# Squared activations of two MLPs: both halves in one buffer, at chosen offsets, and side by side in the second layer

## The chip, the core and the metric

The kernel runs on one core of a Trainium2 chip. The metric is the time of one execution on the device in microseconds (us). Times are read from one profiled execution, and the kernel was timed in further runs without that profile.

## What is computed

The reference is a decoder trunk of two layers on 256 tokens of width 1024, in float32. The first layer mixes tokens by trailing means over 2 to 16 positions, the second by causal attention; both add attention to a memory of 256 rows, and each ends in an MLP with a squared ReLU. Cut to what matters here:

```
for i in range(DEPTH):                       # 2 layers
    u = rms_norm(x, g_mix[i])
    ...                                      # token mixer and memory attention
    x = x + concatenate([tok, mo]) @ w_out[i]
    u = rms_norm(x, g_mlp[i])
    x = x + square(relu(u @ w_ff1[i])) @ w_ff2[i]   # 1024 -> 4096 -> 1024
```

## The kernel before

Every matrix product is done in three parts to keep float32 accuracy. An operand is held as two tiles: `hi`, the value rounded to the type `float32r`, and `lo`, what is left of it. `mm3` (L125 to L128) then adds hi·hi, hi·lo and lo·hi in an accumulator. Weights come from HBM into raw tiles of 512 KB; `split` (L113) makes `hi` on ScalarE (L118, L121) and `lo` on VectorE (L119, L122), 128 partitions by 512 columns each, in a pool of 16 tiles of either kind.

An MLP (`mlp`, L399) works through the 4096 hidden columns in eight groups `g` of 512. `ff1(g)` multiplies the slices of `w_ff1` as stationary operand with the transposed input (`x1T` in the first layer, `x3T` in the second): eight matmuls of 512 columns (L426) and eight of 256 (L428) for each 128 hidden columns. `square` (L402) folds two such accumulators (ScalarE's copy `c` at L407, VectorE's sum `r` at L408), squares the positive part into `h` (L411), rounds it to `hh` on ScalarE (L412) and writes the rest `hl` on VectorE (L413). Each of `hh` and `hl` holds 512 columns: two blocks of 128 hidden units by 256 tokens.

`ff2(g)` multiplies them with `w_ff2`. Here a slice of 128 tokens of `hh` or `hl` is the stationary operand, loaded before each matmul, and 512 columns of the weights are the moving one. A group has 4 hidden blocks × 2 blocks of tokens × 2 halves of the output × 3 parts = 48 matmuls; TensorE loads `hh` for the first two parts (L126, L127) and `hl` for the third (L128). The order on TensorE is ff1(0), ff1(1), ff2(0), ff1(2), ff2(1) and so on, so a group's `hh` and `hl` are written about one group before they are read.

Where tiles lie: `hi`, `lo`, `x1T`, `x3T`, `hh` and `hl` all begin at the same remainder of 512 bytes within a partition, since their sizes are multiples of 512 bytes and a filler tile of 96 values (L232) precedes the pools that hold `hh` and `hl`. Each has 4 buffers of 2048 bytes for `hh` and as many for `hl`, used in turn, so a buffer is written again two groups later.

Of the kernel before, what the change touches and what calls it, by code (L numbers as in the profile page):

```python
# [11 lines left out]
F32R = mybir.dt.float32r  # L12
# [6 lines left out]
P = 128  # L19
# [14 lines left out]
QG, KG = 58, 122  # L34
NSMALL = 186
NWARM = 7
LAG = 2

PLAN = {'x': 6, 'q': 5, 'bw': 7, 'pool': 5, 'mem0': (1, 3, 6, 6),
# [14 lines left out]
def trunk(ctx: ExitStack, tc: tile.TileContext, x, mem, x_t0, x_t, mem_t, small, bands, rope, mask,  # L54
# [13 lines left out]
    def nm(s):  # L68
        uid[0] += 1
        return f"{s}_{uid[0]}"  # L70

    def psum(name="ps"):
        return psp.tile([P, 512], F32, tag="ps", name=nm(name))

    def accum():
        return accp.tile([P, 512], F32, tag="acc", name=nm("acc"))
# [20 lines left out]
    wps = psum("warm")  # L97
    for _ in range(NWARM):
        nc.tensor.matmul(wps, warm[:, :P], warm, start=True, stop=True)
# [3 lines left out]
    def load_raw(src):  # L103

        n = src.shape[1]
        k = src.shape[0] // P
        r = rawp.tile([P, k, n], F32, tag="raw", name=nm("raw"))
        nc.sync.dma_start(r, src.rearrange("(k p) n -> p k n", p=P))
        return r
# [3 lines left out]
    def split(raw, g=None):  # L113
        n = raw.shape[-1]
        hi = wp.tile([P, n], F32R, tag="hi", name=nm("hi"))
        lo = wp.tile([P, n], F32R, tag="lo", name=nm("lo"))
        if g is None:
            nc.scalar.activation(hi, raw, AF.Copy)  # L118
            nc.vector.tensor_tensor(lo, raw, hi.bitcast(F32), op=ALU.subtract)  # L119
        else:  # L120
            last_hi[0] = nc.scalar.activation(hi, raw, AF.Copy, scale=g)  # L121
            nc.vector.scalar_tensor_tensor(lo, raw, g, hi.bitcast(F32), op0=ALU.mult, op1=ALU.subtract)  # L122
        return hi, lo

    def mm3(o, a, b, start, stop):  # L125
        nc.tensor.matmul(o, a[0], b[0], start=start, stop=False)  # L126
        nc.tensor.matmul(o, a[0], b[1], start=False, stop=False)  # L127
        nc.tensor.matmul(o, a[1], b[0], start=False, stop=stop)  # L128
# [20 lines left out]
    def big_t(name):  # L149

        t = tp.tile([P, NKC, 2, S], F32R, tag="t", name=nm(name))
        return t[:, :, 0, :], t[:, :, 1, :], t
# [125 lines left out]
    def later(fn):  # L278
        pend.append(fn)
        while len(pend) > LAG:  # L280
            pend.pop(0)()
# [108 lines left out]
    def mlp_stats():  # L390
        e2 = []
        for b in range(2):
            ms = norm_stats(xr[:, b, :], f"mlp{b}")
            r2 = st.tile([P, 1], F32, tag=f"r2{b}", name=nm("r2"))
            nc.vector.reciprocal(r2, ms)
            e2.append(r2)
        return e2

    def mlp(l, t, hp, finish):  # L399
        acc = []  # L400

        def square(zs, hh, hl):  # L402

            z = hp.tile([P, 2, S], F32, tag="r", name=nm("r"), bufs=2)
            for i in range(2):
                c = hp.tile([P, S], F32, tag="c", name=nm("c"), bufs=2)
                nc.scalar.activation(c, zs[i][:, S:], AF.Copy)  # L407
                nc.vector.tensor_tensor(z[:, i, :], zs[i][:, :S], c, op=ALU.add)  # L408
            z = z.rearrange("p i t -> p (i t)")
            h = hp.tile([P, 512], F32, tag="h", name=nm("h"), bufs=2)  # L410
            nc.vector.scalar_tensor_tensor(h, z, 0.0, z, op0=ALU.max, op1=ALU.mult)  # L411
            nc.scalar.activation(hh, h, AF.Copy)  # L412
            nc.vector.tensor_tensor(hl, h, hh.bitcast(F32), op=ALU.subtract)  # L413

        def ff1(g):
            pieces = []
            for q in range(4):
                raw = load_raw(w_ff1[l][q * 256:(q + 1) * 256, g * 512:(g + 1) * 512])
                for j in range(2):
                    k = 2 * q + j  # L420
                    pieces.append(split(raw[:, j, :], sm[:, GMLP + 8 * l + k:GMLP + 8 * l + k + 1]))

            def steps(o, n, ks):

                for k in ks:
                    nc.tensor.matmul(o, pieces[k][0][:, n * P:(n + 1) * P], t[2][:, k, :, :], start=k == 0, stop=False)  # L426
                for k in ks:
                    nc.tensor.matmul(o[:, :S], pieces[k][1][:, n * P:(n + 1) * P], t[0][:, k, :],  # L428
                                     start=False, stop=k == NKC - 1)

            res = [(hp.tile([P, 512], F32R, tag="hh", name=nm("hh"), bufs=4),
                    hp.tile([P, 512], F32R, tag="hl", name=nm("hl"), bufs=4)) for _ in range(2)]
            if g == 0:
                z = [accum() for _ in range(4)]
                for k0 in (0, 4):
                    for n in range(4):
                        steps(z[n], n, range(k0, k0 + 4))
                for i in range(2):
                    square(z[2 * i:2 * i + 2], *res[i])
                return res  # L440
            for i in range(2):
                z = [psum("step") for _ in range(2)]
                for n in range(2):
                    steps(z[n], 2 * i + n, range(NKC))
                square(z, *res[i])
            return res

        def ff2(g, hs):
            last = g == 7
            if g == 0:  # L450
                acc.extend([[accum(), accum()], [accum(), accum()]])
            held = []

            def go(b, h, f, pieces):
                hh, hl = hs[f // 2]
                o = (f % 2) * S + b * P
                mm3(acc[b][h], (hh[:, o:o + P], hl[:, o:o + P]), pieces[h], g == 0 and f == 0, last and f == 3)

            for f in range(4):
                raw = load_raw(w_ff2[l][g * 512 + f * P:g * 512 + (f + 1) * P, :])  # L460
                held.append([split(raw[:, 0, h * 512:(h + 1) * 512]) for h in range(2)])
                if not last:
                    for b in range(2):
                        for h in range(2):
                            go(b, h, f, held[f])
            if last:
                for h in range(2):
                    for b in range(2):
                        for f in range(4):
                            go(b, h, f, held[f])  # L470
                        finish(b, h, acc[b][h])

        prev = ff1(0)
        r2.extend(mlp_stats())
        for g in range(1, 8):
            cur = ff1(g)
            ff2(g - 1, prev)
            prev = cur
        ff2(7, prev)
# [11 lines left out]
    with tc.tile_pool(name="l0", bufs=1) as lp:  # L491
# [15 lines left out]
        for k in range(0, NKC, 2):  # L507
# [11 lines left out]
            for j in range(2):  # L519
                if k == 0 and j == 1:  # L520
                    evac_split(xt0[:, S:2 * S], xT[0][:, 1, :], xT[1][:, 1, :])
                g = xt0[:, 2 * S + j:2 * S + j + 1] if k == 0 else sm[:, GMIX + k + j:GMIX + k + j + 1]
                p = split(raws[j], g)
# [43 lines left out]
        dhi, dlo, _ = big_t("d")  # L567
# [59 lines left out]
        for l in range(2):  # L627
            g = cp.tile([P, 1], F32, tag=f"mg{l}", name=f"mg{l}")
# [45 lines left out]
    with tc.tile_pool(name="l1", bufs=1) as lp:  # L674
# [6 lines left out]
        for i, (gc, f) in enumerate(((QG, 1.0), (KG, 8.0))):  # L681
            for b in range(2):
                cc, ss = rp[:, b, 0, :], rp[:, b, 1, :]
                g1, g2 = sm[:, gc:gc + 32], sm[:, gc + 32:gc + 64]
                for j, (g, src, sg) in enumerate(((g1, cc, f), (g2, cc, f), (g2, ss, -f), (g1, ss, f))):
                    nc.vector.scalar_tensor_tensor(tcs[:, b, j // 2, i, (j % 2) * 32:(j % 2) * 32 + 32],
                                                   g, sg, src, op0=ALU.mult, op1=ALU.mult)
# [187 lines left out]
```

## Time and profile before

| | us |
|---|---|
| median of 3 timed runs | 562.98 |
| lowest and highest of them | 562.65, 562.99 |
| profiled execution | 562.31 |
| its span, first to last instruction | 560.5 |
| TensorE busy in the span | 552.2 |
| VectorE busy | 397.6 |
| ScalarE busy | 343.2 |

The first layer's MLP fills about 93 to 275 us of the span, the second layer's 376 us to the end. In the rows below PE is TensorE's matmul, PEld its load of a stationary operand (which overlaps matmuls), DVE is VectorE, ACT ScalarE, POOL GpSimd. [...] Names are those of the program, out<-in, with buffer numbers left out.

### The profile page before, as it was taken

What the parts mean: (1) busy time and instruction counts of PE and PEld (TensorE: products, weight loads), DVE (VectorE), ACT (ScalarE), POOL (GpSimd) and SP (SyncE); (2) the same over time, 40 slices, a digit from 0 to 9 for tenths busy, and PEclk for the clock granted to TensorE, in tenths of its full rate; (3) what the DMA queues carried; (4) which work ended last, traced back from release to release, by engine and by line L of the source; (5) the groups of instructions that cost most, each with busy time, mean ns of one, the idle gap of its engine ahead of it and who ended that gap; (6) DMA issues with size and microseconds to landing.
All of it is one profiled execution on the core that took longest, in us unless ns stands there. A gap on an engine that the chain in (4) does not pass through costs nothing.

```text
span 560.5 us, 8156 instructions
## 1 busy us (share of the span) xinstructions
PE 552.2 (99%) x2883; PEld 459.6 (82%) x2883; DVE 397.6 (71%) x795; ACT 343.2 (61%) x658; POOL 24.5 (4%) x27
## 2 busy tenths in 40 slices
PE   7999999999999999999999999999999999999997
PEld 5888788888888888888878777888888888888885
DVE  5888977784765856847969999667768477486542
ACT  6879966574563753755766887656637546466330
POOL 0202110000000000000012112000000000000000
PEclk9999999999999999999999999999999999999999
DMA  8988763645836637549473343355374483574301
GB/s 296 355 307 291 232 195 132 196 142 185 255 122 225 195 146 260 161 143 295 132 229 113 108 143 118 116 178 160 114 262 143 160 291 111 198 238 135 117 0 75
DMA packets 46408, 101.94 MB, mean 182 GB/s; under 512 B 3488, under 2 KB 11168, under 8 KB 46368
## 3 DMA queue, kind: packets, MB, share of 16 engines
q1 hardware_dynamic: 46224, 101.17, 55.5%
q8 instruction: 22, 0.36, 0.3%
q10 hardware_dynamic: 144, 0.26, 0.1%
q14 instruction: 18, 0.15, 0.1%
HBM read 100.37 MB, written 1.05 MB: 181 GB/s over the span
## 4 chain that ended last, share of the span: by engine, by line
PE 91%; DVE 3%; ACT 2%; POOL 1%; DMA 1%; issue 1%; ACTq 0%; DVEq 0%
PE step L426 18%; PE acc L126 18%; PE acc L127 18%; PE acc L128 18%; PE step L428 10%; PE acc L426 3%; PE av_out L342 1%; PE acc L428 1%; PE exp_t L306 1%; POOL r L172 1%; PE transpose L145 1%; PE tok_scores L723 1%; ACT hi L121 1%; DMA raw<-in_w_in_pool_dram 1%; DVE lo L122 1%
## 5 line engine op out<-in xcount | busy, mean ns | idle before, releaser
L122 DVE SCALAR_TENSOR_TENSOR lo<-raw,sm,hi 128x512 fp32r<-128x512 f32 x210 | 149.4, 749 | 31.6 <-ACT hi L121 18.1
L121 ACT ACTIVATE hi<-raw,sm 128x512 fp32r<-128x512 f32 x210 | 139.6, 718 | 32.3 <-PE acc L128 29.9
L118 ACT ACTIVATE hi<-raw 128x512 fp32r<-128x512 f32 (+1 forms) x152 | 92.2, 628 | 45.8 <-PE acc L128 40.5
L119 DVE TENSOR_TENSOR lo<-raw,hi 128x512 fp32r<-128x512 f32 (+1 forms) x152 | 97.2, 689 | 19.7 <-ACT hi L118 19.7
L126 PE MATMUL acc<-hi,hh 128*128 128x512 f32 x256 | 99.9, 390 | 0.0
L128 PE MATMUL acc<-hi,hl 128*128 128x512 f32 x256 | 99.8, 390 | 0.0
L127 PE MATMUL acc<-lo,hh 128*128 128x512 f32 x256 | 99.8, 390 | 0.0
L408 DVE TENSOR_TENSOR r<-step,c 128x256 f32<-128x256 f32 x56 | 23.7, 423 | 57.7 <-ACT c L407 57.7
L407 ACT ACTIVATE c<-step 128x256 f32<-128x256 f32 x56 | 21.3, 380 | 68.8 <-PE step L428 68.8
L128 PEld LDWEIGHTS acc<-hi,hl 128*128 128x128 f32 x256 | 48.1, 188 | 10.0
L426 PE MATMUL step<-x1T,hi 128*128 128x512 f32 x224 | 55.9, 392 | 0.0
L426 PE MATMUL step<-x3T,hi 128*128 128x512 f32 x224 | 55.9, 392 | 0.0
L126 PEld LDWEIGHTS acc<-hi,hh 128*128 128x128 f32 x256 | 48.1, 188 | 9.5
L127 PEld LDWEIGHTS acc<-lo,hh 128*128 128x128 f32 x256 | 48.1, 188 | 9.5
L426 PEld LDWEIGHTS step<-x3T,hi 128*128 128x128 f32 x224 | 40.7, 189 | 7.5
L426 PEld LDWEIGHTS step<-x1T,hi 128*128 128x128 f32 x224 | 40.7, 189 | 7.5
L428 PEld LDWEIGHTS step<-x3T,lo 128*128 128x128 f32 x224 | 30.6, 190 | 2.2
L428 PEld LDWEIGHTS step<-x1T,lo 128*128 128x128 f32 x224 | 30.5, 190 | 2.2
L126 PE MATMUL acc<-hi,x2T 128*128 128x512 f32 x80 | 32.1, 401 | 0.0
L128 PE MATMUL acc<-hi,x2T 128*128 128x512 f32 x80 | 31.7, 396 | 0.0
L127 PE MATMUL acc<-lo,x2T 128*128 128x512 f32 x80 | 31.6, 395 | 0.0
L428 PE MATMUL step<-x3T,lo 128*128 128x256 f32 x224 | 31.2, 282 | 0.0
(155 smaller groups left out, 778.3 us busy)
## 6 DMA issues: line engine op xcount, KB each, us to landing
raw<-in_w_ff_dram SPq DMA_DIRECT2D x128, 512.0 KB, 4.8
raw<-in_w_out_dram SPq DMA_DIRECT2D x16, 512.0 KB, 4.4
raw<-in_w_in_moba_dram SPq DMA_DIRECT2D x24, 256.0 KB, 4.2
raw<-in_w_mem_kv_dram SPq DMA_DIRECT2D x8, 512.0 KB, 4.6
raw<-in_w_in_moba_dram SPq DMA_DIRECT2D x8, 512.0 KB, 4.8
raw<-in_w_in_pool_dram SPq DMA_DIRECT2D x7, 512.0 KB, 6.5
xr<-in_x_dram SPq DMA_DIRECT2D x2, 512.0 KB, 8.2
raw<-in_mem_t_dram SPq DMA_DIRECT2D x4, 256.0 KB, 6.6
```

The source lines that it names most:

```text
L118: nc.scalar.activation(hi, raw, AF.Copy)
L119: nc.vector.tensor_tensor(lo, raw, hi.bitcast(F32), op=ALU.subtract)
L121: last_hi[0] = nc.scalar.activation(hi, raw, AF.Copy, scale=g)
L122: nc.vector.scalar_tensor_tensor(lo, raw, g, hi.bitcast(F32), op0=ALU.mult, op1=ALU.subtract)
L126: nc.tensor.matmul(o, a[0], b[0], start=start, stop=False)
L127: nc.tensor.matmul(o, a[0], b[1], start=False, stop=False)
L128: nc.tensor.matmul(o, a[1], b[0], start=False, stop=stop)
L145: nc.tensor.transpose(ps[:, c * P:(c + 1) * P], src[:, (c0 + c) * P:(c0 + c + 1) * P], ident)
L407: nc.scalar.activation(c, zs[i][:, S:], AF.Copy)
L408: nc.vector.tensor_tensor(z[:, i, :], zs[i][:, :S], c, op=ALU.add)
L426: nc.tensor.matmul(o, pieces[k][0][:, n * P:(n + 1) * P], t[2][:, k, :, :], start=k == 0, stop=False)
L428: nc.tensor.matmul(o[:, :S], pieces[k][1][:, n * P:(n + 1) * P], t[0][:, k, :], start=False, stop=k == NKC - 1)
```

## The change

The two tiles become one of 9 × 128 values (4608 bytes), one for each of the four buffers `j` = 2·(g mod 2) + i. Within it the halves begin at an offset from the table `RES`, in bytes.

In the first layer (`l` = 0) `hh` is 512 contiguous columns at that offset and `hl` the next 512; the four offsets are 224, 160, 16 and 240 bytes. In the second layer (`l` = 1) the buffer is 512 pairs: `hh` takes the even places and `hl` the odd ones, so that the two halves of a value lie side by side, and neighbouring columns of `hh` are 8 bytes apart; the offsets are 0, 64, 128 and 192 bytes. Since a buffer's size is a multiple of 512 bytes and its pool begins where it did, these offsets are also the distances from the remainder at which the weights begin.

```
+RES = (224, 160, 16, 240, 0, 64, 128, 192)
...
-            res = [(hp.tile([P, 512], F32R, tag="hh", name=nm("hh"), bufs=4),
-                    hp.tile([P, 512], F32R, tag="hl", name=nm("hl"), bufs=4)) for _ in range(2)]
+            res = []
+            for i in range(2):
+                j = 2 * (g % 2) + i
+                u = hp.tile([P, 9 * P], F32R, tag=f"hb{j}", name=nm("hb"), bufs=1)
+                o = RES[4 * l + j] // 4
+                if l:
+                    w = u[:, o:o + 1024].rearrange("p (n two) -> p n two", two=2)
+                    res.append((w[:, :, 0], w[:, :, 1]))
+                else:
+                    res.append((u[:, o:o + 512], u[:, o + 512:o + 1024]))
```

The instructions of each engine stand in the same order as before, with the same shapes, and each waits for the same engines. What differs is the addresses of `hh` and `hl`, and in the second layer the step of two elements with which ScalarE and VectorE write them, VectorE reads `hh` at L413, and TensorE loads them.

## Rows read from the trace of the kernel before

**Rows 1.** the page: busy us of each engine, and the granted clock in tenths

```profile
span 560.5 us, 8156 instructions
...
PE 552.2 (99%) x2883; PEld 459.6 (82%) x2883; DVE 397.6 (71%) x795; ACT 343.2 (61%) x658; POOL 24.5 (4%) x27
...
PEclk9999999999999999999999999999999999999999
```

**Rows 2.** who TensorE waited for, whole span: us in total, times, longest us

```profile
PE acc L126 <- ACT hi L121: 1.6, 1, 1.6
PE mem_kv_finish L255 <- DVE kn L242: 1.3, 2, 0.8
PE warm L99 <- DVE warm L94: 1.2, 1, 1.2
```

**Rows 3.** the chain of work that ended last, shares of the span by engine

```profile
PE 91%; DVE 3%; ACT 2%; POOL 1%; DMA 1%; issue 1%; ACTq 0%; DVEq 0%
```

**Rows 4.** groups by line in the second MLP, 376 to 560.5 us: TensorE

```profile
line engine op names shapes xcount | busy us, mean ns | idle before us <-releasers
...
L127 PEld LDWEIGHTS acc<-lo,hh 128*128 128x128 f32 x128 | 24.1, 188 | 4.7
L126 PEld LDWEIGHTS acc<-hi,hh 128*128 128x128 f32 x128 | 24.1, 188 | 4.8
L128 PEld LDWEIGHTS acc<-hi,hl 128*128 128x128 f32 x128 | 24.0, 188 | 5.0
```

**Rows 5.** timeline of TensorE's matmuls around one ff2 block: start us, us, instruction, count

```profile
503.37 1.12 PE L428 MATMUL step<-x3T,lo 128*128 128x256 f32 x8
504.32 2.00 PE L426 MATMUL step<-x3T,hi 128*128 128x512 f32 x8
506.16 1.12 PE L428 MATMUL step<-x3T,lo 128*128 128x256 f32 x8
...
512.70 0.40 PE L126 MATMUL acc<-hi,hh 128*128 128x512 f32 x1
...
514.09 0.39 PE L126 MATMUL acc<-hi,hh 128*128 128x512 f32 x1
...
523.38 0.39 PE L128 MATMUL acc<-hi,hl 128*128 128x512 f32 x1
523.61 1.98 PE L426 MATMUL step<-x3T,hi 128*128 128x512 f32 x8
```

**Rows 6.** timeline of TensorE's weight loads in that block

```profile
514.09 0.19 PEld L127 LDWEIGHTS acc<-lo,hh 128*128 128x128 f32 x1
```

**Rows 7.** timeline of TensorE, a matmul beside which nothing is loaded

```profile
339.18 0.39 PE L126 MATMUL acc<-hi,x2T 128*128 128x512 f32 x1
...
339.38 0.20 PEld L710 LDWEIGHTS qk_evac<-ident,rot 128*128 128x128 f32 x2 [0.23 <-ACT hi L118]
339.41 0.41 PE L710 MATMUL qk_evac<-ident,rot 128*128 128x128 f32 x2
```

**Rows 8.** groups by line in the second MLP: ScalarE and VectorE

```profile
L118 ACT ACTIVATE hi<-raw 128x512 fp32r<-128x512 f32 x64 | 39.2, 630 | 21.8 <-PE acc L128 19.2 <-PE acc L426 1.9
...
L413 DVE TENSOR_TENSOR hl<-h,hh 128x512 fp32r<-128x512 f32 x16 | 11.1, 691 | 5.0 <-ACT hh L412 4.9
...
L412 ACT ACTIVATE hh<-h 128x512 fp32r<-128x512 f32 x16 | 10.0, 628 | 9.1 <-DVE h L411 9.1
```

**Rows 9.** busy us of each engine in the two MLPs' stretches

```profile
core 0: us, PE busy (x) PEld busy (x) DVE busy (x) ACT busy (x) POOL busy (x), PEclk, DMA share, GB/s
...
376.00:560.50 184.50, 180.70 (x919) 153.77 (x917) 114.55 (x193) 93.31 (x170) 0.00 (x0) 1.00 0.47 155
```

**Rows 10.** timelines of VectorE and TensorE: the last hl, and its buffer's first reader

```profile
538.72 0.69 DVE L413 TENSOR_TENSOR hl<-h,hh 128x512 fp32r<-128x512 f32 x1
...
545.66 0.39 PE L126 MATMUL acc<-hi,hh 128*128 128x512 f32 x1
...
547.02 0.39 PE L126 MATMUL acc<-hi,hh 128*128 128x512 f32 x1
```

## The prediction

> **What bounds the kernel now.** I read the busy shares first. TensorE is busy for 552.2 of 560.5 us, at the full granted clock in every slice, with VectorE at 71% and ScalarE at 61% [rows 1]. Busy does not yet mean bound, so the second view is the list of what TensorE waited for: three entries, 4.1 us in total, on lines 99, 126 and 255, and at none of them is a squared activation the operand waited for [rows 2]. The chain that ended last is TensorE for 91% of the span [rows 3]. So only an edit that alters the spacing of matmuls can move the end by much, and the question is what this one does to that spacing.
>
> The change touches two kinds of instruction in each MLP: ScalarE's and VectorE's writes of the two halves (`hh` at L412, `hl` at L413, 16 each per layer), and the weight loads of the second matrix product, in which a 128-column slice of `hh` or `hl` is the stationary operand (L126 to L128). There are 384 of these per layer: 256 with `hh`, 128 with `hl` [rows 4]. Each is followed by one matmul of 512 columns. No engine's order and no kind of wait changes, so there is no moved step to price, only durations and what lies behind them.
>
> **How fast the product runs now.** In the timeline of TensorE I take the starts of one block of 48 of these matmuls [rows 5]. From 514.09 to 523.38 there are 41 intervals: 9.29 us / 41 = 226.6 ns each. The first six intervals, from 512.70 to 514.09, come straight after the shorter matmuls of L428 and take 1.39 us, or 231.7 ns each. The whole block, 512.70 to 523.61, takes 10.91 us; 48 × 226.6 = 10.88. Only 0.03 us of a block is above its own steady pace.
>
> Is 226.6 ns a floor, or is it itself the result of weight loads that get in the way of the matmul being streamed? At 339.18 a 512-column matmul of L126 starts, and the next weight load begins only at 339.38, since it waited for another engine; the next matmul starts at 339.41 [rows 7]. The interval is 0.23 us although nothing was loaded for the first 0.20 us of it. The same 0.23 with and without a load beside it: I take 226.6 ns as the matmul's own time. That limits the gain: 16 blocks × 0.03 us = 0.5 us, under 0.1% of the time.
>
> **How much room a weight load has.** The load of the next matmul is issued when the present one starts (514.09 for both) [rows 5, 6]. The 256-column matmuls of L428 show how long a load keeps its unit occupied: eight of them, each with a load of its own, start at 503.37 and the next group at 504.32 [rows 5], 0.95 us / 8 = 119 ns. A load therefore occupies at most 119 ns, although the records show about 190 ns for one [rows 4], a length that evidently overlaps its successor. Under a 512-column matmul it has 226.6 − 119 = 108 ns to spare.
>
> **The edits, one by one.**
> (a) Second layer, stride of two elements in 384 weight loads. The trace has no weight load with a stride. Lower bound of its cost: nothing, if the load takes up to 1.9 times as long (226.6 / 119), because it stays under the matmul. Upper bound: a load of twice the length, 238 ns, then sets the interval: (238 − 226.6) × 384 = 4.4 us. I take nothing, since the spare time covers all but a full doubling. What the cover hides is 384 × 119 = 46 us of loading.
>
> [...]
>
> (b) First layer, 384 contiguous loads whose buffers begin 224, 160, 16 and 240 bytes off the grid of 512 bytes on which all weight tiles and, so far, all of `hh` and `hl` begin. Slices now differ by multiples of 512 bytes, and the steady block [rows 5] runs through all of them at one pace; nothing in the trace shows a finer offset. Lower bound: all stalls after L428 vanish, −0.25 us (8 blocks × 0.03). Upper bound: every matmul pays what the first six of a block pay, 231.7 − 226.6 = 5.1 ns, × 384 = 2.0 us. I take nothing: 41 of 47 intervals of the block are at the floor.
>
> [...]
>
> (c) ScalarE's and VectorE's strided writes in the second layer: 16 × 628 ns and 16 × 691 ns now [rows 8]. Between unchanged and doubled, this adds 0 to 10.0 us on ScalarE and 0 to 11.1 us on VectorE. In 376 to 560.5 us they are busy 93.31 and 114.55 of 184.5 us [rows 9], so even doubled they stay at 103 and 126. The cover is the distance between writing and reading: the last `hl` of the kernel is written at 538.72 and its buffers are first read seven matmuls into the block from 545.66, at 547.02 [rows 10], some 7.6 us later; all other buffers have at least the block in between. Behind these instructions on their queues stand the splits of weights (L118, L119) and the copies that free the accumulators (L407); ScalarE waits for TensorE there, 19.2 us in front of L118 in this stretch [rows 8], and TensorE never for it in the MLP [rows 2]. Taken at nothing. Should the cover go, the cost would be the 0.7 us of the last such instruction, once.
>
> (d) One buffer for both halves in place of two: it is reused two groups later, as before; no new wait.
>
> **Sum.** The profiled execution took 562.31 us, 1.8 us more than its span of 560.5; the median of the three timed runs is 562.98, 0.67 above it. Terms: 0 + 0 + 0 + 0, with ends of −0.5 and +6.4 us. Forecast: 563.0 us.
>
> **Rivals.**
> R1, slower: offsets decide whether a load and a matmul that run together stall. Place: the 384 pairs of the first layer, and perhaps those of the second, where the load now walks through memory twice as fast. Price: the 231.7 ns of the first six intervals as a lasting pace, 2.0 us per layer; by the eight L426 matmuls after L428 (504.32 to 506.16, 1.84 us / 8 = 230 ns) 1.3 us. So 564.3 to 565.0 for one layer, up to 567.0 for both. It decides once the stall lasts instead of dying out. For it: stalls exist, with the same instructions, and depend on something as fine as the moment of a load's start. Against: they die out within six matmuls.
> R2, slower: the strided load takes about twice as long, 4.4 us in the second layer alone: 567.4. It decides from 226.6 ns on. For it: twice as many bytes are passed over for the same 128 columns. Against: the 108 ns of room.
> [...]
> R4: the edit does nothing, because the addresses do not matter and the stride is free. That is the forecast itself.
>
> **How the numbers follow.** Forecast (with R4) 0.51, R1 0.28, R2 0.16, R3 0.05. A measurement of this kernel tells about 0.2%, or 1.1 us, from no change. Faster by more 0.05 (R3; the 0.5 us of stalls is not enough), within 0.2% 0.51, slower 0.44 (R1 and R2). The range runs from 562.3 (the forecast with every stall gone) to 567.2, which takes in R1 whole and most of R2, and leaves out R3 and the upper end of R2, some 0.13.
>
> **What would show it.** [...] The durations of L412 and L413 in the second layer show (c), and the list of TensorE's waits must still have no entry on L126 to L128 for `hh` or `hl`. The forecast is wrong if either layer's blocks of 48 take more than 10.95 us each, or if a wait for L412 or L413 appears on TensorE.

## The result and the profile after

The changed kernel takes 566.50 us (median of 4 runs, 566.12 to 567.63) against 562.97 us for the kernel before (4 runs, 562.65 to 562.99): a ratio of 1.0072 with a 95% interval of 1.0058 to 1.0085, 3.5 us slower. That lies in the range, but the central forecast, no change, was wrong. What happened is the rival R1, in both layers: in the first by the offsets, in the second already by the stride.

The page of the kernel after, its parts on busy time, the granted clock and the chain that ended last:

```profile
span 565.8 us, 8156 instructions
...
PE 557.5 (99%) x2883; PEld 463.2 (82%) x2883; DVE 397.6 (70%) x795; ACT 343.2 (61%) x658; POOL 24.5 (4%) x27
...
PEclk9999999999999999999999999999999999999999
...
PE 91%; DVE 3%; ACT 2%; POOL 1%; DMA 1%; issue 1%; ACTq 0%; DVEq 0%
```

Beside [rows 1, 3] only TensorE differs. VectorE and ScalarE are busy exactly as long as before, the granted clock shows as full in every slice, the chain has the same shares. TensorE is busy 5.3 us longer with the same 2883 matmuls, and the span has grown by the same 5.3 us.

Who TensorE waited for in the kernel after (us in total, times, longest):

```profile
PE acc L129 <- ACT hi L124: 1.7, 1, 1.7
PE mem_kv_finish L258 <- DVE kn L245: 1.3, 2, 0.8
PE warm L102 <- DVE warm L97: 1.2, 1, 1.2
```

These are the three entries of [rows 2], three lines further down in the code (L126 to L128 are now L129 to L131, L426 is L429, L412 and L413 are L415 and L416). There is no new wait. Matmuls with nothing to wait for stand further apart. (A matmul recorded at 0.39 us at 523.38 is followed by the next at 523.61 [rows 5]; in a stream one costs the distance between two starts, here 0.23 us.)

Where? Timelines of TensorE, first and last matmul of either MLP (first of L429, last of L131), after:

```profile
96.31 1.08 PE L429 MATMUL acc<-x1T,hi 128*128 128x512 f32 x4
...
276.39 0.39 PE L131 MATMUL acc<-hi,hb 128*128 128x512 f32 x1
...
382.99 1.08 PE L429 MATMUL acc<-x3T,hi 128*128 128x512 f32 x4
...
561.64 0.39 PE L131 MATMUL acc<-hi,hb 128*128 128x512 f32 x1
```

and the same four in the kernel before:

```profile
94.79 1.07 PE L426 MATMUL acc<-x1T,hi 128*128 128x512 f32 x4
...
272.93 0.40 PE L128 MATMUL acc<-hi,hl 128*128 128x512 f32 x1
...
379.60 1.08 PE L426 MATMUL acc<-x3T,hi 128*128 128x512 f32 x4
...
556.31 0.39 PE L128 MATMUL acc<-hi,hl 128*128 128x512 f32 x1
```

The first MLP takes 180.08 us instead of 178.14, the second 178.65 instead of 176.71: 1.94 us more in each. The other 1.5 us by which the profiled spans differ had passed before the first MLP began (96.31 against 94.79). That stretch is not touched by the change. In the eight runs below that leave it alone as well, the MLP began between 1.2 us earlier and 0.8 us later than in the trace of before, whatever the edit. What differs lies in the first 13 us. TensorE starts the first projection at 6.0 us before and 6.1 us after and runs on without a pause; its 512-column matmuls stand 0.43 us apart at first, up to 8.7 us before and up to 12.2 us after, and 0.23 us from then on. (The trace's records of the granted clock begin, at full, at 8.9 us before and at 12.2 us after; what it was until then no record shows, and the page counts that time as full.) Eight intervals more at 0.43 us cost 1.6 us. That is probably why the profiled execution, at 567.63, is the longest of the four. The comparisons that decide below use the length of an MLP or of one block, which this start does not enter.

Within the MLPs it is almost all in the second product: the intervals that start with one of its matmuls add up to 1.79 us more in the first layer and 1.85 in the second. The rest is in the L429 matmuls (229.4 to 230.2 and 229.9 ns). Timelines of TensorE after: one `ff2` block in the second layer, then one in the first.

```profile
517.28 0.40 PE L129 MATMUL acc<-hi,hb 128*128 128x512 f32 x1
517.52 0.40 PE L130 MATMUL acc<-lo,hb 128*128 128x512 f32 x1
...
528.44 0.85 PE L429 MATMUL step<-x3T,hi 128*128 128x512 f32 x3
```

```profile
119.13 0.39 PE L129 MATMUL acc<-hi,hb 128*128 128x512 f32 x1
...
130.32 0.86 PE L429 MATMUL step<-x1T,hi 128*128 128x512 f32 x3
```

From the first row of a block to the L429 behind it are 48 matmuls: 11.16 us here against 10.91 in [rows 5], and 11.19 in the first layer. The blocks alternate, since even and odd groups use different buffers: 11.19 and 11.10 us in the first layer, 11.10 and 11.16 in the second. Over the six full blocks of a layer the intervals average 233.3, 233.0, 233.4 and 228.9 ns for the first layer's buffers (offsets 224, 160, 16 and 240) and 232.8, 229.9, 231.9 and 233.2 for the second's (0, 64, 128 and 192). So a pace like that of the first six matmuls of a block before (231.7 ns) now holds through most blocks to the end. The exception is the buffer at 240, the second half of this block:

```profile
141.50 0.39 PE L129 MATMUL acc<-hi,hb 128*128 128x512 f32 x1
...
147.11 0.39 PE L129 MATMUL acc<-hi,hb 128*128 128x512 f32 x1
...
152.60 0.62 PE L429 MATMUL step<-x1T,hi 128*128 128x512 f32 x2
```

At offset 16 the first 24 matmuls take 5.61 us, 233.8 ns each; at 240 the other 24 take 5.49 us, 228.8 ns each.

### The profile page after: what moved, and what is told of

Its sections match the earlier page's. It is cut to its first block, busy times and chain, and to the rows that moved or that the text cites. A ratio compares the mean times of both kernels' runs of the same rounds, so it can differ in the third digit from the quotient of the medians.

```text
span 565.8 us, 8156 instructions
## 1 busy us (share of the span) xinstructions
PE 557.5 (99%) x2883; PEld 463.2 (82%) x2883; DVE 397.6 (70%) x795; ACT 343.2 (61%) x658; POOL 24.5 (4%) x27
## 4 chain that ended last, share of the span: by engine, by line
PE 91%; DVE 3%; ACT 2%; POOL 1%; DMA 1%; issue 1%; ACTq 0%; DVEq 0%
PE step L429 18%; PE acc L129 18%; PE acc L130 18%; PE acc L131 18%; PE step L431 9%; PE acc L429 3%; PE av_out L345 1%; PE acc L431 1%; PE exp_t L309 1%; POOL r L175 1%; PE transpose L148 1%; PE tok_scores L734 1%; DMA raw<-in_w_in_pool_dram 1%; ACT hi L124 1%; DVE lo L125 1%
## 5 line engine op out<-in xcount | busy, mean ns | idle before, releaser
L130 PE MATMUL acc<-lo,hb 128*128 128x512 f32 x256 | 101.0, 395 | 0.0
L129 PE MATMUL acc<-hi,hb 128*128 128x512 f32 x256 | 100.9, 394 | 0.0
L131 PE MATMUL acc<-hi,hb 128*128 128x512 f32 x256 | 100.9, 394 | 0.0
L131 PEld LDWEIGHTS acc<-hi,hb 128*128 128x128 f32 x256 | 48.9, 191 | 10.3
L129 PEld LDWEIGHTS acc<-hi,hb 128*128 128x128 f32 x256 | 49.1, 192 | 9.9
L130 PEld LDWEIGHTS acc<-lo,hb 128*128 128x128 f32 x256 | 48.9, 191 | 9.7
L429 PE MATMUL step<-x1T,hi 128*128 128x512 f32 x224 | 56.1, 392 | 0.0
L429 PE MATMUL step<-x3T,hi 128*128 128x512 f32 x224 | 56.0, 392 | 0.0
L429 PEld LDWEIGHTS step<-x1T,hi 128*128 128x128 f32 x224 | 40.7, 189 | 7.7
L429 PEld LDWEIGHTS step<-x3T,hi 128*128 128x128 f32 x224 | 40.6, 189 | 7.7
L129 PE MATMUL acc<-hi,x2T 128*128 128x512 f32 x80 | 32.1, 401 | 0.0
L131 PE MATMUL acc<-hi,x2T 128*128 128x512 f32 x80 | 31.7, 396 | 0.0
L130 PE MATMUL acc<-lo,x2T 128*128 128x512 f32 x80 | 31.6, 395 | 0.0
L415 ACT ACTIVATE hb<-h 128x512 fp32r<-128x512 f32 x32 | 20.7, 648 | 17.6 <-DVE h L414 17.6
```

## Experiments

Below, **distance** is a difference of byte offsets within a partition, mod 256: that of a slice being loaded less that of the operand streamed meanwhile. The load beside a matmul is that of the next one [rows 5, 6]: beside L129 and L131 (moving `hi`) `hh` is loaded, beside L130 (moving `lo`) `hl`. Before, all distances in this product were 0. Distances are worked out from the program's tile sizes and offsets; no trace shows an address. Where a kernel was executed several times, its ratio is given with a 95% interval; a kernel executed once has none and is judged by its trace.

### Each layer alone

`e1_off0` keeps the offsets of the first layer and puts the second back on contiguous halves at offset 0; `e2_pair1` keeps the pairs of the second layer and puts offset 0 into the first.

```
e1: -RES = (224, 160, 16, 240, 0, 64, 128, 192)
    +RES = (224, 160, 16, 240, 0, 0, 0, 0)        # and no pairs in either layer
e2: +RES = (0, 0, 0, 0, 0, 64, 128, 192)          # pairs in the second layer as in the change
```

> One buffer for both halves in both layers, contiguous; the first layer's buffers begin 224, 160, 16 and 240 bytes off the weights' grid as in the changed kernel, the second layer's on the grid. Theory O (a load whose addresses are off the grid of the operand being streamed beside it stalls that matmul by some 5 ns, pairs or not): first-layer interval of the second product 231 to 233 ns, second-layer interval 226.7 to 227.2, time 563.0 + 1.9 = 564.9 us. Theory S (only the stride of the pairs costs, the first layer's +1.9 us came with it by another route): 563.0 us and 227 ns in both layers. Theory P (one buffer in place of two costs, whatever the offsets): 231 to 233 ns in both layers, 566.5 us.

> The first layer's buffers on the weights' grid, contiguous; the second layer's as in the changed kernel (pairs, offsets 0, 64, 128, 192 bytes). Theory O: second-layer interval 230 to 234 ns for all four buffers, first layer 227 to 228, time 563.0 + 1.9 = 564.9 us. Theory S: the same, 564.9 us. Theory P: 566.5 us.

Measured: 564.74 against 562.89 us for `e1_off0`, ratio 1.0029 [1.0020, 1.0039]; 564.60 for `e2_pair1`, 1.0031 [1.0020, 1.0041]. One block in the first and one in the second layer of `e1_off0`:

```profile
118.36 0.39 PE L129 MATMUL acc<-hi,hb 128*128 128x512 f32 x1
...
129.55 0.63 PE L429 MATMUL step<-x1T,hi 128*128 128x512 f32 x2
```

```profile
405.06 0.40 PE L129 MATMUL acc<-hi,hb 128*128 128x512 f32 x1
...
415.96 1.30 PE L429 MATMUL step<-x3T,hi 128*128 128x512 f32 x5
```

and one in the second layer of `e2_pair1`:

```profile
402.69 0.39 PE L129 MATMUL acc<-hi,hb 128*128 128x512 f32 x1
...
413.80 1.55 PE L429 MATMUL step<-x3T,hi 128*128 128x512 f32 x6
```

11.19 and 10.90 us, and 11.11. The MLPs take 180.10 and 176.71 us in `e1_off0`, 178.15 and 178.64 in `e2_pair1`: each half of the change costs its own layer what it costs in the whole (1.9 us), and the other layer nothing. By the timed runs 1.85 + 1.71 = 3.56 us, where the whole change has 3.5.

### One buffer instead of two

`e3_pack` leaves only the repacking: one tile per buffer, contiguous halves, all offsets 0.

```
+RES = (0, 0, 0, 0, 0, 0, 0, 0)                   # and no pairs in either layer
```

> One buffer for both halves in both layers, contiguous, all on the weights' grid (offset 0). Theory O and theory S: 226.7 to 228 ns in both layers and the time of the kernel before, 563.0 us within 0.4. Theory P: 566.5 us.

Measured: 562.85 against 562.89 us, ratio 1.0002 [0.9993, 1.0012]. A block of its second layer:

```profile
402.82 0.40 PE L129 MATMUL acc<-hi,hb 128*128 128x512 f32 x1
...
413.73 1.52 PE L429 MATMUL step<-x3T,hi 128*128 128x512 f32 x6
```

10.91 us, as before. The repacking is free, as the prediction's term (d) had it.

### Which offsets

`e4_map` has contiguous halves in both layers and other offsets in each buffer.

```
+RES = (32, 48, 96, 256, 0, 64, 128, 192)         # and no pairs in either layer
```

> Contiguous in both layers. First layer at offsets 32, 48, 96 and 256 bytes, second layer at 0, 64, 128 and 192, the places of the pairs without their stride. Theory O with a period of 256 bytes: 227 ns at 0 and 256, 230 to 235 at each of the other six, time 563.0 + 0.75 x 1.9 x 2 = 565.9 us. Theory S: 227 ns for all of the second layer, 564.4 us or less. If offsets count by rows of 64 bytes alone: 64, 128, 192 and 256 at 227 ns, 32, 48 and 96 above 230, 564.4 us.

Measured: 566.04 against 562.89 us, ratio 1.0054 [1.0036, 1.0072]. In an odd group of the first layer the first 24 matmuls read the buffer at 96, the other 24 that at 256:

```profile
140.55 0.39 PE L129 MATMUL acc<-hi,hb 128*128 128x512 f32 x1
...
146.16 0.40 PE L129 MATMUL acc<-hi,hb 128*128 128x512 f32 x1
...
147.55 0.40 PE L129 MATMUL acc<-hi,hb 128*128 128x512 f32 x1
...
150.96 0.39 PE L129 MATMUL acc<-hi,hb 128*128 128x512 f32 x1
```

From 140.55 to 146.16 at offset 96: 5.61 us / 24 = 233.8 ns. After the change to 256 the pace recovers within six matmuls: from 147.55 to 150.96 it is 3.41 us / 15 = 227.3 ns. Mean intervals over the six full blocks of a layer: 232.8 ns at 32, 233.3 at 48, 234.0 at 96, 233.2 at 64, 232.2 at 128, 233.2 at 192; 227 in the median at 0 and at 256. With the change's own 16, 160, 224 and 240, ten distances other than 0 have been seen, and all stall: nine by 5.6 to 7.4 ns over 226.6, and 240 by 2.3. So being off is not all that counts: 240, 16 bytes short of the grid, costs less than half as much as 16 bytes past it (233.4). 256 is as good as 0, so in this product the remainder by 256 bytes counts.

### Place or distance

`e5_shift32` takes the kernel before and puts a filler of 32 bytes ahead of all its tiles, so that everything moves and no distance changes.

```
+    cp.tile([P, 8], F32, tag="shift", name="shift")
```

> The kernel before with every weight tile, every transposed activation and every hh and hl moved on by 32 bytes together (their distance to each other stays 0). If the distance between the loaded and the streamed operand decides: 226.7 to 228 ns and 562.9 us within 0.4. If the place in memory itself decides (all of them now begin at 64 in place of 32 of a 256-byte row): 231 to 234 ns and 566.5 us or more, since all loads of the kernel are then off.

Measured: 562.66 against 562.86 us, ratio 1.000 [0.999, 1.001]. A block:

```profile
118.24 0.40 PE L127 MATMUL acc<-hi,hh 128*128 128x512 f32 x1
...
129.15 1.07 PE L427 MATMUL step<-x1T,hi 128*128 128x512 f32 x4
```

10.91 us. Moving everything by 32 bytes changes nothing, where the same 32 bytes for one side alone cost 6 ns an interval in `e4_map`: the common remainder matters, and this move of the place does not.

### One of three loads off

`e6_half` moves only one half in each layer: in the first `hl` (by 64, 128, 192, 32), in the second `hh`. In the first layer two loads in three are then at distance 0.

```
+RES = (64, 128, 192, 32, 64, 128, 192, 32)
...
-                    w = u[:, o:o + 1024].rearrange("p (n two) -> p n two", two=2)
-                    res.append((w[:, :, 0], w[:, :, 1]))
+                    res.append((u[:, o:o + 512], u[:, 576:1088]))
...
-                    res.append((u[:, o:o + 512], u[:, o + 512:o + 1024]))
+                    res.append((u[:, :512], u[:, o + 512:o + 1024]))
```

> Contiguous halves in one buffer. First layer: hh on the grid, hl off it by 64, 128, 192 or 32 bytes. Second layer: hl on the grid, hh off it by these. Local theory (a matmul stalls when the load running beside it is off, and no other does): first layer, only the matmuls beside which hl is loaded at 231 to 235 ns, the others at 227, MLP +0.65 us; second layer, the two thirds beside which hh is loaded stalled, MLP +1.3 us; 564.9 us in all. Spreading theory (one stall moves the start of the next load and so the next matmul stalls too): 231 to 235 ns for all parts of both layers, +1.9 us each, 566.7 us.

Measured in one execution: 566.65 against 562.86 us; MLPs 179.74 and 178.69. In the first layer:

```profile
118.39 0.40 PE L129 MATMUL acc<-hi,hb 128*128 128x512 f32 x1
...
129.50 0.84 PE L429 MATMUL step<-x1T,hi 128*128 128x512 f32 x3
```

and in the second:

```profile
404.78 0.40 PE L129 MATMUL acc<-hi,hb 128*128 128x512 f32 x1
...
415.94 1.30 PE L429 MATMUL step<-x3T,hi 128*128 128x512 f32 x5
```

11.11 us with one load of three off in every block, 11.16 and 11.10 in turn with two. By parts (L129, L130, L131) the intervals of the first layer's full blocks are 230.3, 232.3 and 232.1 ns: the stall does not stay with the matmul beside the shifted load, it lengthens all three. So one load off in three costs nearly as much as all three, and the matmul whose record shows a delay need not be the one beside which the load was off.

### Does a strided load take longer

Under a 512-column matmul, 226.6 ns from start to start, a load's own length of at most 119 ns [rows 5] is hidden. `e7_narrow` splits every matmul of the second product into two of 256 columns, each with its load, so that a much longer load would set the pace; offsets 0 in even groups of the first layer, 64 and 128 in odd ones, pairs in the second.

```
+RES = (0, 0, 64, 128, 0, 64, 128, 192)
...
-                mm3(acc[b][h], (hh[:, o:o + P], hl[:, o:o + P]), pieces[h], ...)
+                for c in (0, 256):
+                    mm3(acc[b][h][:, c:c + 256], (hh[:, o:o + P], hl[:, o:o + P]),
+                        (pieces[h][0][:, c:c + 256], pieces[h][1][:, c:c + 256]), ...)
```

> Each matmul of the second product done as two of 256 columns, each with a load of its own (the output is unchanged), so that a load no longer has room under its matmul. First layer contiguous at offsets 0, 0, 64, 128; second layer pairs at 0, 64, 128, 192. Interval by the load that bounds it: contiguous at offset 0 some 120 ns as in L428. Pairs: 120 to 128 ns if the strided load takes as long as a contiguous one or the 7 ns longer that its records show; 230 to 240 ns if it takes twice as long (the rival of the prediction, hidden under 512 columns). The time grows by about 768 x 13 ns = 10 us in the first case.

One execution: 570.85 against 562.86 us. Blocks of 96 matmuls at offset 0, at 64 and 128, and in pairs:

```profile
116.38 0.28 PE L129 MATMUL acc<-hi,hb 128*128 128x256 f32 x1
...
127.90 1.32 PE L429 MATMUL step<-x1T,hi 128*128 128x512 f32 x5
```

```profile
139.07 0.28 PE L129 MATMUL acc<-hi,hb 128*128 128x256 f32 x1
...
150.42 0.86 PE L429 MATMUL step<-x1T,hi 128*128 128x512 f32 x3
```

```profile
428.37 0.29 PE L129 MATMUL acc<-hi,hb 128*128 128x256 f32 x1
...
439.93 0.86 PE L429 MATMUL step<-x3T,hi 128*128 128x512 f32 x3
```

11.52 us / 96 = 120.0 ns, 11.35 / 96 = 118.2 and 11.56 / 96 = 120.4. Had a strided load taken twice as long, the last would be near 240. R2 is excluded: the load is not longer by more than about 2 ns (against the contiguous 118.2 at 64 and 128), and yet the matmul beside it is slowed.

What pairs cost under 512 columns is another thing: 229.9 to 233.2 ns an interval, by buffer, in the second layer of the kernel after, against 226.6.

### Pairs without an offset

`e10_pairs` has pairs in both layers, all at offset 0 in the first.

```
+RES = (0, 0, 0, 0, 16, 32, 48, 96)
...
-                if l:
+                if True:
```

> Pairs in both layers: first layer all four buffers at offset 0, second layer at 16, 32, 48 and 96 bytes. If a strided load stalls the matmul whatever its offset, because it walks away from where a contiguous load would be: 230 to 235 ns in both layers, +1.9 us each, 566.6 us. If offset 0 is clean for pairs too and the 232.5 ns at offset 0 in the changed kernel came over from its off-grid neighbours: 227 to 228 ns in the first layer and +1.9 us in the second alone, 564.8 us.

One execution: 567.49 against 562.85 us; MLPs 180.36 (+2.22) and 179.04 (+2.33). A block at offset 0:

```profile
118.35 0.39 PE L129 MATMUL acc<-hi,hb 128*128 128x512 f32 x1
...
129.53 0.85 PE L429 MATMUL step<-x1T,hi 128*128 128x512 f32 x3
```

11.18 us, with 233.3 ns an interval once the first are past. The stride stalls the stream even where the first byte of the buffer is on the grid (227 in the median for contiguous halves at 0, `e4_map`). The run shows only the cost, not why.

### Other operands

`e8_tmap` keeps the squared activations as before and makes the rows of the transposed activations 16 bytes longer, so that slice `k` of `x2T` and `x3T` lies 16·`k` bytes off, and that of `x1T`, which is in the pool's second buffer, 128 + 16·`k`. (The filler of 96 values shrinks to 32, to make room.)

```
-        t = tp.tile([P, NKC, 2, S], F32R, tag="t", name=nm(name))
+        t = tp.tile([P, NKC, 2 * S + 4], F32R, tag="t", name=nm(name))
+        t = t[:, :, :2 * S].rearrange("p k (two s) -> p k two s", two=2)
```

> The kernel before with 16 bytes left free after each of the eight slices of the transposed activations, so that slice k lies 16 k bytes off the weights' grid (second buffer: 128 + 16 k). They are the stationary operand of the projections and the streamed one of ff1. Distance theory: in the projections the matmuls beside which slice 0 of the first buffer is loaded stay at 227 ns, the others go to 230 to 235 ns (some 460 x 5.5 ns = 2.5 us); in ff1 L426 goes from 230 to 231 to 235 ns (+0 to 2 us); 565 to 567.5 us. If in ff1 the shorter matmuls of L428 (119 ns, where 113 is seen when nothing is loaded) stall by distance and not by the load's own length, some offset gives 113 to 116 there.

One execution: 566.02 against 562.86 us, of which 2.1 us passed before the first MLP; most of that is again a longer stretch at 0.43 us a matmul. Where no wait interrupts them, the 512-column matmuls with `x2T` as stationary operand run at 231 to 233 ns on average at every distance, 231.4 at distance 0, against 227 to 229 in the kernel before: I had expected 227 there. `e6_half` suggests why it is more, since there too a load at distance 0 stalled among neighbours that were off. In `ff1`, where the transposed activations are the moving operand, the 512-column matmuls of L426's kind went from 229.4 to 233.0 ns in the first layer and 230.8 in the second, where they differ by place: 225 to 226 ns at distances 144 and 192, 228 to 236 at the others. Those of 256 columns, at 119.0 ns before, ran at 115 to 117 ns at three distances in a row (80, 96 and 112 in `x1T`) and at 117.5 on average there. So the 119 ns that the prediction read as a load's length holds some stall too. The trace of before shows it as well: the first interval of each group of eight on L428 is 113.4 ns on average, with a load beside it that starts when it starts. (The expectation took 113 ns for a matmul beside which nothing is loaded; the trace has a load there.) The effect is not peculiar to the squared activations.

### Tries at a faster kernel, and what they left open

If only distances decide, all `lo` tiles may lie 96 bytes off all `hi` tiles: the load beside each 512-column matmul of the second product (`hh` beside `hi`, `hl` beside `lo`) stays at distance 0, and the short matmuls of L428's kind get a better one. `e9_lo96` moves the `lo` weights, `hl` and the `lo` halves of the activations; `e9_lo112` was to do so by 112 bytes.

```
+X = 24                                           # e9_lo112: 28
...
+            wp.tile([P, X], F32R, tag="glo", name=nm("glo"), bufs=1)
...                                              # fillers behind lo and before hl left out
+        t = tp.tile([P, 2 * n + 64], F32R, tag="t", name=nm(name))
+        both = t[:, :2 * (n + X)].rearrange("p (two q) -> p two q", two=2)[...]
...
-        junk = st.tile([P, D], BF16, tag="junk", name=nm("junk"), bufs=1)
+        junk = st.tile([P, D], BF16, tag="sq", name=nm("junk"), bufs=1)
```

> A try to use what the map showed. All lo tiles (weights, transposed activations, hl) lie 96 bytes off all hi tiles, so that a load beside a 512-column matmul always has distance 0 (hi beside hi, lo beside lo), and only in L428 of ff1, where 256 columns of the hi input are streamed beside a load of lo weights, the distance is 96. Distance theory: the second product stays at 226.7 to 228 ns in both layers, L426 at 230, and L428 falls from 119 to 115 to 117 ns; 448 x 3 ns = 1.3 us, so 561.5 us. If the distance must be 0 for every pair, or one off-grid load disturbs the following matmuls for good, L426 and the second product go to 231 to 235 ns and the time to 566 us or more.

> The same with 112 bytes, the offset at which the map showed 115.8 ns in L428. Distance theory: 561.5 us, L428 at 115 to 117 ns. If the offsets within L428 differ by the place of the slice and not by the distance, both kernels stay at 118 to 120 ns there and at 562.9 us.

Measured: 574.18 against 562.45 us, ratio 1.0215 [1.0191, 1.0239], and 574.42, 1.0221 [1.0203, 1.0239]. Both are slower. TensorE's list of waits in `e9_lo96` has entries that were never there:

```profile
PE transpose L151 <- DVE xr L396: 2.1, 2, 1.1
...
PE acc L435 <- ACT x3T L139: 1.4, 1, 1.4
PE acc L435 <- ACT x1T L139: 1.4, 1, 1.4
```

They come with the layout that the edit needed (two separate halves of `t`, a scratch tile shared with `sq`), which also delayed the first MLP by 4.8 us and lengthened the stretch between the MLPs by 3.6. In the profiled execution the mean granted clock was 0.990 besides; in that of `e9_lo112`, whose list has the same three entries, it was 1.000. But the product did not run as hoped either: blocks of 11.03 us instead of 10.91, three successive intervals averaging 231.1, 232.7 and 225.5 ns, together 689 where the kernel before has 682 over a whole block. The 256-column matmuls fell from 119.0 to 117.3 ns on average, just short of the 115 to 117 that was expected, but those of 512 columns in `ff1` rose from 229.4 to 231.6, which takes back more. The blocks of `e9_lo112` take 11.10 us. That its fillers of 112 and 144 bytes gave the distances meant, 0 and 112, was not shown, so I take no answer on 112 from it.

`e11_loonly` then moved the `lo` weight tiles alone by 96 bytes, so that one load in three is off, that of `hl` beside `lo`.

```
+            wp.tile([P, 24], F32R, tag="glo", name=nm("glo"), bufs=1)
...
-    mkp.tile([P, 96], F32, tag="gap", name="gap")
+    mkp.tile([P, 32], F32, tag="gap", name="gap")
```

> The kernel before with all lo weight tiles 96 bytes off the grid and nothing else moved: hh, hl and the transposed activations stay on it. Beside a streamed hi tile every load is at distance 0; beside a streamed lo tile hl is loaded at distance 160. In the kernel with hl and the lo halves moved along (distance 0 everywhere in the second product) three matmuls took 231.1 + 232.7 + 225.5 = 689 ns against 680 on the grid. If the distance to the operand streamed beside the load decides, this kernel must be worse than that one, 695 ns or more for three; if a clean stream needs everything on one grid, streamed operands too, it is no different, 685 to 693 ns. MLP +1.5 to +3 us per layer.

One execution: 566.89 against 562.85 us; MLPs 179.51 and 178.18. A block:

```profile
118.62 0.40 PE L131 MATMUL acc<-hi,hh 128*128 128x512 f32 x1
...
129.72 0.63 PE L431 MATMUL step<-x1T,hi 128*128 128x512 f32 x2
```

11.10 us, three intervals in 694 ns. That falls between the two expectations: `e9_lo96`, where every load is at distance 0, is 4 ns better in three intervals than `e11_loonly`, where one in three is not (689.4 against 693.8 over a block), but still nearly 8 ns worse than one remainder for all tiles (681.7). So a load at distance 0 to its own stream is not enough for the full pace. Nor does the stall hang on the writes of `hh` and `hl`: in `e11_loonly` they lie where they lay before. Whether distances alone count, or one remainder common to all that TensorE reads, isn't settled. No version was faster than the kernel before.

## Why the prediction was wrong in the middle and right at the edge

**What bounds the kernel**: right. TensorE's spacing decides, no wait appeared, and the whole difference is between starts of matmuls.

**226.6 ns as the matmul's own time** [rows 5, 7]: it stood as the best pace of a stream. No block of 48 took less than 10.89 us in any run (the second layer of `e8_tmap`; 48 × 226.6 ns is 10.88), so the faster rival, R3, found no support, though intervals of 225.5 ns on average beside one line in `e9_lo96` show that 226.6 is no strict floor for a single one. The interval without a load could not have decided it: the matmul at 339.41 starts 0.03 us after its own late load at 339.38, so that load may have set its start.

**Term (b), the offsets: this step failed.** It took 0 from ends of −0.25 and 2.0 us, since 41 of 47 intervals of a block were at the floor. But all those loads lay at distance 0, so the row could not speak of any other distance, as the sentence ahead of it conceded. Two rows bore on matmuls that are disturbed, the first six intervals and the L426 matmuls behind L428, and both said 230 to 232 ns. The upper end was worked out from the right row: 2.0 us stood there, 1.94 was measured. So close a hit holds some luck, since the price came from stalls at distance 0, and of the four offsets three cost 6 to 7 ns and one 2. The mistake was to read a small number of stalls under one layout as a sign of a small stall under another. That they die out within six matmuls, the argument against R1, holds only on the grid; `e4_map` shows the recovery at 256 and none at 96.

**Term (a), the pairs**: the length was right and the conclusion wrong. The room of 108 ns under a matmul exists and the strided load fits in it (`e7_narrow`, 120.4 against 120.0 ns). The sum treated a load as either hidden or longer than its cover. It can be hidden and still slow what covers it: 1.94 us, R1's price a second time, even at offset 0 (`e10_pairs`). The upper end of 4.4 us was built on the wrong mechanism, and R2 with it.

**A load beside a matmul.** The measured 226.6 ns become 232 to 234 with the same load off the grid (`e4_map`), and 228.9 at 240 in the kernel after. So a load off the grid slows the matmuls of this product by 2 to 7 ns, and (b) is zero only where all operands share one remainder.

**Term (c), the strided writes**: right in its consequence. Groups by line in the second MLP after:

```profile
L130 PEld LDWEIGHTS acc<-lo,hb 128*128 128x128 f32 x128 | 24.9, 195 | 4.5
...
L416 DVE TENSOR_TENSOR hb<-h,hb 128x512 fp32r<-128x512 f32 x16 | 11.0, 690 | 5.3 <-ACT hb L415 5.2
...
L415 ACT ACTIVATE hb<-h 128x512 fp32r<-128x512 f32 x16 | 10.7, 670 | 9.1 <-DVE h L414 9.1
```

ScalarE's write takes 670 ns instead of 628 [rows 8], 0.7 us over the layer; VectorE's, with a strided input and output, 690 against 691. The cover of some 7 us behind each stands, and no wait for L415 or L416 appeared. The recorded length of a load grew from 188 to 195 ns [rows 4]; in the first layer it stayed at 188 to 189 while the intervals grew as much, so the stall does not need a longer load.

**Term (d)**: right, by `e3_pack`.

**The range**: 566.5 lies in it because of R1's price for both layers (567.0), not because of the forecast. Two of its statements do not follow from the sum: 563.0 less 0.5 is 562.5 and not 562.3, and R2's only price, 567.4, lies above 567.2, so the range does not take in most of R2.

**Its own sign of being wrong** pointed the right way: blocks over 10.95 us in both layers (11.10 to 11.19). Their intervals, 229 to 234 ns by buffer, are neither the 226.6 of the forecast nor the 238 of a load twice as long. The chance of 0.28 for R1 was too low for a case whose price was the only one taken from stalls that the trace shows.

**What stays open**: why the remainder by 256 bytes counts, why 240 costs so much less than 16, what in a load off the grid slows the matmul beside it, and the 689 and 694 ns of the last section. The traces of the MLPs add up to 3.9 us, the medians to 3.5; I have not followed the difference of 0.4, which is within what the start of the first MLP moves from run to run.

## What to carry to other kernels

When TensorE is the bound and every 512-column float32r matmul has a load of its own, let all stationary and moving tiles begin at the same remainder of 256 bytes, and keep the stationary slices contiguous: in this kernel one load in three elsewhere already costs most of the penalty (blocks of 11.11 us in `e6_half`, 10.91 with none off, 11.10 to 11.19 with all). A hidden operation is not yet a free one; before taking its cost at zero, ask whether the trace holds any row in which the new form runs beside the work that hides it. Where it does not, give weight to the end that comes from stalls seen in the trace.

## Hardware behaviour that I had not expected

- Of eleven distances between load and stream in the second product (0, 16, 32, 48, 64, 96, 128, 160, 192, 224, 240 bytes, mod 256) only 0 runs at 227 ns, and only where all operands share one remainder (`e9_lo96`, at 0 without that: three intervals in 689 ns, 682 before); 240 lies at 229, the others at 232 to 234.
- The stall spreads: with one load in three off by 32 to 192 bytes, all three intervals are 230 to 232 ns on average.
- Matmuls of 256 columns, each with a contiguous load, are slightly faster with an offset: 118.2 against 120.0 ns in the split second product, 117.3 against 119.0 in `ff1` of `e9_lo96`.
- A weight load with a step of 8 bytes takes no longer than a contiguous one at offset 0 (120.4 against 120.0 ns), and VectorE does not mind the step (690 against 691), but ScalarE's write does (670 against 628).
